# One square, one sum and one root per large piece in a streaming p = 2 pooling kernel

## The chip, the cores and the metric

The kernel runs on one core of a Trainium2 chip. The metric is device time in microseconds (us) of one execution. All times of kernels are medians; a profile is of one single run. A ratio is the mean time of one kernel's runs over that of the other's runs of the same rounds, so it is not quite the ratio of the two medians that stand beside it.

## The reference

```python
x = randn(32, 256, 4096) float32;  p = 2.0;  kernel_size = 4
for i in range(1024):
    window = np.abs(x[:, :, 4*i : 4*i+4]) ** p
    result[:, :, i] = np.mean(window, axis=-1) ** (1.0 / p)
```

For p = 2 each output is the square root of a quarter of the sum of four squares. 134.2 MB are read and 33.6 MB written, and each input element is used once.

## The kernel before

A partition holds 13184 columns of x at a time, in one of three buffers ("slots"). ScalarE squares in place, VectorE adds groups of four into an output buffer, and ScalarE takes roots there. A load fills a slot and is worked on in three pieces. Two loads make a group, which is stored as one block; there are two output buffers. A small odd piece comes first, and the last loads are smaller.

```python
slots = [[(W, [4416, 4384, 4384])]] * 18          # W = 13184: one load, three pieces
slots += [[(6592, [3296, 3296])] * 2, [(6592, [3296, 3296]), (4216, [2112, 2104])]]
X_SLOTS, O_SLOTS = 3, 2
groups = [2] * 9 + [3, 1]
late = {7, 8, 9, 10}                              # these are stored from the sync queue, at the end
FINE, ENDS, LAG = range(22), (), 1                # FINE: loads whose every piece has its own root
PAIRS = 16                                        # from this load on: two adds instead of a reduce
# ... (loads, blocks and buffers cut)
for i in range(n):
    s, _, w, chunks = loads[i]
    while ahead < n and loads[ahead][0] < s + X_SLOTS:
        load(ahead); ahead += 1                   # waits, on the queue, until its slot is free
    # ... (choice of the output buffer cut)
    for step in chunks:
        v = xs[i][:, c:c + step]
        nc.scalar.activation(out=v, in_=v, func=Act.Square)
        total_sum(ots[g][:, summed:summed + step // k], v, i)
        while pending and pending[0][0] <= done - LAG:
            root(*pending.pop(0)[1:])             # a root comes one piece late; at a group's end, the store
        # ... (counting cut)
        if ends or i in FINE or (i in ENDS and c == w):
            pending.append((done - 1, g, ots[g][:, rooted:summed], ends))
```

Of the kernel before, what the change touches and what calls it, by code (L numbers as in the profile page):

```python
# [1 line left out]

# [4 lines left out]


@with_exitstack
def kernel(  # L10
    ctx: ExitStack,
    tc: tile.TileContext,
    x: bass.AP,
    p: float,
    kernel_size: int,
    out: bass.AP,
):








    nc = tc.nc

    assert float(p) == 2.0, "kernel specialized for p == 2"
    k = int(kernel_size)
    assert k == 4, "kernel specialized for kernel_size == 4"  # L30

    P = nc.NUM_PARTITIONS
    fp32 = mybir.dt.float32
    Act = mybir.ActivationFunctionType
    xf = x.rearrange("b c l -> (b c l)")
    of = out.rearrange("b c l -> (b c l)")
    total = xf.shape[0] // P

    W, O_W = 13184, 6592
    X_SLOTS, O_SLOTS = 3, 2  # L40
    slots = [[(W, [4416, 4384, 4384])]] * 18
    slots += [[(6592, [3296, 3296])] * 2, [(6592, [3296, 3296]), (4216, [2112, 2104])]]
    ODD = 840
    groups = [2] * 9 + [3, 1]
    late = {7, 8, 9, 10}
    in_x = {9: (2, 0), 10: (2, 4944)}
    FINE, ENDS, LAG = range(22), (), 1
    PAIRS = 16


    loads = [(s, sum(w for w, _ in slot[:j]), *slot[j]) for s, slot in enumerate(slots)
             for j in range(len(slot))]
    n = len(loads)
    assert sum(w for _, _, w, _ in loads) + ODD == total

    firsts = [sum(groups[:g]) for g in range(len(groups))]
    assert sum(groups) == n
    group_of = [g for g, count in enumerate(groups) for _ in range(count)]
    columns = [sum(w for _, _, w, _ in loads[firsts[g]:firsts[g] + groups[g]])
               for g in range(len(groups))]  # L60

    x_pool = ctx.enter_context(tc.tile_pool(name="x_pool", bufs=1))
    o_pool = ctx.enter_context(tc.tile_pool(name="o_pool", bufs=1))

    x_tiles = [x_pool.tile([P, W], fp32, name=f"xt{j}") for j in range(X_SLOTS)]
    o_tiles = [o_pool.tile([P, O_W], fp32, name=f"ot{j}") for j in range(O_SLOTS)]
    ctx.enter_context(tc.manual_schedule())

    def block(flat, g, div):
        at, width = sum(columns[:g]) * P // div, columns[g] * P // div  # L70
        return flat[at:at + width].rearrange("(p w) -> p w", p=P)

    xs = {}

    def load(i):
        s, at, w, _ = loads[i]
        v = x_tiles[s % X_SLOTS][:, at:at + w]
        g = group_of[i]
        src = sum(loads[j][2] for j in range(firsts[g], i))
        nc.sync.dma_start(out=v, in_=block(xf, g, 1)[:, src:src + w])  # L80
        xs[i] = v

    ots = {}

    def store(g, queue):
        queue.dma_start(out=block(of, g, k), in_=ots[g])  # L86

    def root(g, o, ends):
        nc.scalar.activation(out=o, in_=o, func=Act.Sqrt, scale=1.0 / k)  # L89
        if ends and g not in late:  # L90
            store(g, nc.scalar)

    def total_sum(o, v, i):
        add = mybir.AluOpType.add
        if i < PAIRS:
            nc.vector.tensor_reduce(  # L96
                out=o, in_=v.rearrange("p (n j) -> p n j", j=k),
                axis=mybir.AxisListType.X, op=add,
            )
            return  # L100

        q = v.rearrange("p (n j) -> p n j", j=k)
        front = v[:, 0:v.shape[1] // 2]
        h = front.rearrange("p (n j) -> p n j", j=2)
        nc.vector.tensor_tensor(out=h, in0=q[:, :, 0:2], in1=q[:, :, 2:4], op=add)  # L105
        nc.vector.tensor_tensor(out=o, in0=h[:, :, 0], in1=h[:, :, 1], op=add)  # L106


    Q = 120
    odd = ODD * P // Q  # L110
    t = o_tiles[1][0:Q, 0:odd]
    nc.sync.dma_start(out=t, in_=xf[(total - ODD) * P:total * P].rearrange("(p w) -> p w", p=Q))  # L112
    ahead = 0
    while ahead < n and loads[ahead][0] < X_SLOTS:
        load(ahead)
        ahead += 1
    nc.scalar.activation(out=t, in_=t, func=Act.Square)  # L117
    o = o_tiles[1][0:Q, odd:odd + odd // k]
    nc.vector.tensor_reduce(  # L119
        out=o, in_=t.rearrange("p (n j) -> p n j", j=k),  # L120
        axis=mybir.AxisListType.X, op=mybir.AluOpType.add,
    )
    nc.scalar.activation(out=o, in_=o, func=Act.Sqrt, scale=1.0 / k)  # L123
    nc.scalar.dma_start(
        out=of[(total - ODD) * P // k:total * P // k].rearrange("(p w) -> p w", p=Q), in_=o,
    )
    pending = []
    done = 0
# [3 lines that stand above are left out]
            load(ahead)  # L132
            ahead += 1
        g = group_of[i]
        if i == firsts[g]:
            t, first = (o_tiles[g % O_SLOTS], 0) if g not in in_x else (x_tiles[in_x[g][0]], in_x[g][1])
            ots[g] = t[:, first:first + columns[g] // k]
            summed = rooted = 0
        assert sum(chunks) == w
        c = 0  # L140
        for step in chunks:
            v = xs[i][:, c:c + step]
            nc.scalar.activation(out=v, in_=v, func=Act.Square)  # L143
            total_sum(ots[g][:, summed:summed + step // k], v, i)
            while pending and pending[0][0] <= done - LAG:
                root(*pending.pop(0)[1:])
            done += 1
            c += step
            summed += step // k
            ends = summed == columns[g] // k  # L150
            if ends or i in FINE or (i in ENDS and c == w):
                pending.append((done - 1, g, ots[g][:, rooted:summed], ends))
                rooted = summed
    for job in pending:
        root(*job[1:])
    for g in sorted(late):
        store(g, nc.sync)


# [1 line left out]
_INS = ['x', 'p', 'kernel_size']  # L161
_OUTS = [((32, 256, 1024), 'float32')]

_NUMBERS = {'p': 2.0, 'kernel_size': 4}


# [26 lines left out]
```

## Time and profile before

| | kernel before |
|---|---|
| time, beside the changed kernel | 394.81 us (394.58 to 395.49, 6 runs) |
| span of the profile | 392.8 us |
| packet time of both DMA queues | 99.2% of the time of the core's 16 DMA engines |
| ScalarE (ACT), VectorE (DVE) busy | 292.5 us, 271.8 us |

Read the packet time first, and the engines against it. The last number is the median time in us from issue to landing:

```profile
xt<-in_x_dram SPq DMA_DIRECT2D x18, 6592.0 KB, 39.9
out_dram<-ot ACTq DMA_DIRECT2D x7, 3296.0 KB, 27.6
```

A load has 6592 KB, 128 rows of 52,736 bytes.

### The profile page before, as it was taken

How to read it: one execution, taken by the hardware profiler on the slowest of the kernel's cores; microseconds unless marked ns; L12 is line 12 of the kernel's file. 1: busy time of each engine (PE TensorE's matmuls, PEld its weight loads, DVE VectorE, ACT ScalarE, POOL GpSimd, SP SyncE). 2: the span in 40 equal slices, each digit the busy share in tenths (PEclk: the TensorE clock that was granted, in tenths of full speed). 3: DMA queues.
4: the chain of work that ended last, by engine and by line, in shares of the span. 5: the costliest groups of instructions: out<-in, count | busy, mean ns of one | idle time of the engine just before them, and what ended most of it. 6: DMA issues, size and time to landing. Idle time of an engine off the chain costs nothing.

```text
span 392.8 us, 341 instructions
## 1 busy us (share of the span) xinstructions
DVE 271.8 (69%) x77; ACT 292.5 (74%) x128; POOL 0.2 (0%) x4
## 2 busy tenths in 40 slices
DVE  1059989594959495949594959495949494778781
ACT  3088987776776777677867786868586859899990
POOL 0000000000000000000000000000000000000000
DMA  9999999999999989999999999999999999999997
GB/s 361 420 429 446 446 446 384 430 470 430 389 432 473 430 387 435 467 430 422 432 435 430 427 435 427 430 435 459 459 404 430 459 438 430 395 430 432 429 432 315
DMA packets 5024, 167.79 MB, mean 427 GB/s; under 512 B 558, under 2 KB 678, under 8 KB 926
## 3 DMA queue, kind: packets, MB, share of 16 engines
q1 hardware_dynamic: 3879, 144.04, 85.2%
q10 hardware_dynamic: 1143, 23.73, 14.0%
q14 instruction: 2, 0.02, 0.0%
HBM read 134.22 MB, written 33.55 MB: 427 GB/s over the span
## 4 chain that ended last, share of the span: by engine, by line
DMA 62%; ACT 21%; DVE 10%; issue 4%; SPq 0%; ACTq 0%
DMA xt<-in_x_dram 62%; ACT xt L143 17%; DVE ot L96 8%; ACT ot L89 3%; ACT xt L89 1%; DVE xt L105 1%; DVE xt L106 0%; ACTq L86 0%; SPq L80 0%; SPq L112 0%; ACTq L89 0%
## 5 line engine op out<-in xcount | busy, mean ns | idle before, releaser
L143 ACT ACTIVATE xt<-xt 128x4384 f32<-128x4384 f32 (+4 forms) x62 | 229.6, 3705 | 85.1 <-DMA xt<-in_x_dram 81.9
L96 DVE TENSOR_REDUCE ot<-xt 128x1096 f32<-128x4384 f32 (+1 forms) x48 | 227.0, 4731 | 90.1 <-ACT xt L143 89.8
L89 ACT ACTIVATE ot<-ot 128x1096 f32<-128x1096 f32 (+1 forms) x54 | 59.8, 1107 | 1.8 <-DVE ot L96 1.1
L105 DVE TENSOR_TENSOR xt<-xt 128x1648 f32<-128x1648 f32 (+4 forms) x14 | 28.4, 2032 | 16.0 <-ACT xt L143 16.0
L89 ACT ACTIVATE xt<-xt 128x824 f32<-128x824 f32 (+2 forms) x8 | 6.5, 817 | 1.9 <-DVE xt L106 1.9
L106 DVE TENSOR_TENSOR ot<-xt 128x1096 f32<-128x1096 f32 (+1 forms) x6 | 7.8, 1303 | 0.2
L106 DVE TENSOR_TENSOR xt<-xt 128x824 f32<-128x824 f32 (+2 forms) x8 | 7.5, 939 | 0.3
L119 DVE TENSOR_REDUCE ot<-ot 120x224 f32<-120x896 f32 x1 | 1.1, 1086 | 5.7 <-ACT ot L117 5.7
L117 ACT ACTIVATE ot<-ot 120x896 f32<-120x896 f32 x1 | 0.9, 949 | 2.7 <-DMA ot<-in_x_dram 2.7
L117 ACT ACT_TABLE_LOAD x1 | 1.3, 1283 | 0.7 <-PEq L174 0.7
L123 ACT ACT_TABLE_LOAD x1 | 1.3, 1283 | 0.0
L123 ACT ACTIVATE ot<-ot 120x224 f32<-120x224 f32 x1 | 0.4, 389 | 0.0
L174 POOL MEMSET const-bfloat16-1.0<- 128x1 bf16 x1 | 0.1, 101 | 0.0
L174 POOL MEMSET const-uint8-127<- 128x1 uint8 x1 | 0.1, 101 | 0.0
L174 POOL MEMSET const-float32-0.0<- 128x1 f32 x1 | 0.1, 99 | 0.2 <-issue 0.2
L174 POOL MEMSET const-float32-1.0<- 128x1 f32 x1 | 0.1, 99 | 0.0
## 6 DMA issues: line engine op xcount, KB each, us to landing
xt<-in_x_dram SPq DMA_DIRECT2D x18, 6592.0 KB, 39.9
out_dram<-ot ACTq DMA_DIRECT2D x7, 3296.0 KB, 27.6
xt<-in_x_dram SPq DMA_DIRECT2D x3, 3296.0 KB, 29.4
out_dram<-ot SPq DMA_DIRECT2D x2, 3296.0 KB, 30.0
out_dram<-xt SPq DMA_DIRECT2D x1, 2472.0 KB, 10.4
xt<-in_x_dram SPq DMA_DIRECT2D x1, 2108.0 KB, 26.8
out_dram<-xt SPq DMA_DIRECT2D x1, 527.0 KB, 7.1
ot<-in_x_dram SPq DMA_DIRECT2D x1, 420.0 KB, 4.0
```

What stands on the lines that cost most here:

```text
L89: nc.scalar.activation(out=o, in_=o, func=Act.Sqrt, scale=1.0 / k)
L96: nc.vector.tensor_reduce(out=o, in_=v.rearrange("p (n j) -> p n j", j=k), axis=mybir.AxisListType.X, op=add,)
L105: nc.vector.tensor_tensor(out=h, in0=q[:, :, 0:2], in1=q[:, :, 2:4], op=add)
L106: nc.vector.tensor_tensor(out=o, in0=h[:, :, 0], in1=h[:, :, 1], op=add)
L117: nc.scalar.activation(out=t, in_=t, func=Act.Square)
L119: nc.vector.tensor_reduce(out=o, in_=t.rearrange("p (n j) -> p n j", j=k), axis=mybir.AxisListType.X, op=mybir.AluOpType.add,)
L123: nc.scalar.activation(out=o, in_=o, func=Act.Sqrt, scale=1.0 / k)
L143: nc.scalar.activation(out=v, in_=v, func=Act.Square)
L174: nc = _bacc.Bacc("TRN2", target_bir_lowering=False, num_devices=1)
```

## The change

The intent is to pay the fixed cost of an instruction once for a whole load: one square and one sum for each load, one root for each store. The two-add form of the sum starts one load earlier, at load 15. Waits that follow from others are declared away. The odd piece is squared on VectorE, and its root and store stay on ScalarE.

```diff
-    slots = [[(W, [4416, 4384, 4384])]] * 18
-    slots += [[(6592, [3296, 3296])] * 2, [(6592, [3296, 3296]), (4216, [2112, 2104])]]
+    slots = [[(W, [W])]] * 17 + [[(W, [6592, 6592])]]
+    slots += [[(6592, [6592]), (6592, [6592])], [(6592, [6592]), (4216, [2112, 2104])]]
-    FINE, ENDS, LAG = range(22), (), 1
-    PAIRS = 16
+    FINE, ENDS, LAG = {21}, {19, 20}, 1
+    PAIRS = 15
+    def follows(ins, before):
+        for b in before:
+            tc.declare_no_dep(ins.ins, b.ins, reason="follows from other waits")
... (calls of follows() after each square, sum and root cut)
-    nc.scalar.activation(out=t, in_=t, func=Act.Square)
+    nc.vector.tensor_tensor(out=t, in0=t, in1=t, op=mybir.AluOpType.mult)
```

More of the change, by code (lines that the diff above doesn't have):

```diff
@@ L73 @@
     xs = {}
+    by_load = []
     def load(i):
@@ L83 @@
     ots = {}
+    stores = {}
+    by_act = []
+    sums = []
+    def follows(ins, before):
+        for b in before:
+            tc.declare_no_dep(ins.ins, b.ins, reason="follows from other waits")
     def store(g, queue):
-        queue.dma_start(out=block(of, g, k), in_=ots[g])
+        stores[g] = queue.dma_start(out=block(of, g, k), in_=ots[g])
     def root(g, o, ends):
-        nc.scalar.activation(out=o, in_=o, func=Act.Sqrt, scale=1.0 / k)
+        r = nc.scalar.activation(out=o, in_=o, func=Act.Sqrt, scale=1.0 / k)
+        follows(r, by_act[:-1] + list(stores.values()))
+        by_act.append(r)
         if ends and g not in late:
@@ L95, in total_sum @@
         if i < PAIRS:
-            nc.vector.tensor_reduce(
+            r = nc.vector.tensor_reduce(
                 out=o, in_=v.rearrange("p (n j) -> p n j", j=k),
@@ L99, in total_sum @@
             )
+            follows(r, sums[:-1])
+            sums.append(r)
             return
@@ L104, in total_sum @@
         h = front.rearrange("p (n j) -> p n j", j=2)
-        nc.vector.tensor_tensor(out=h, in0=q[:, :, 0:2], in1=q[:, :, 2:4], op=add)
-        nc.vector.tensor_tensor(out=o, in0=h[:, :, 0], in1=h[:, :, 1], op=add)
+        r = nc.vector.tensor_tensor(out=h, in0=q[:, :, 0:2], in1=q[:, :, 2:4], op=add)
+        follows(r, sums[:-1] + by_load)
+        r = nc.vector.tensor_tensor(out=o, in0=h[:, :, 0], in1=h[:, :, 1], op=add)
+        follows(r, sums[:-1])
+        sums.append(r)
     Q = 120
@@ L123 @@
     nc.scalar.activation(out=o, in_=o, func=Act.Sqrt, scale=1.0 / k)
-    nc.scalar.dma_start(
+    stores["odd"] = nc.scalar.dma_start(
         out=of[(total - ODD) * P // k:total * P // k].rearrange("(p w) -> p w", p=Q), in_=o,
@@ L142 @@
             v = xs[i][:, c:c + step]
-            nc.scalar.activation(out=v, in_=v, func=Act.Square)
+            r = nc.scalar.activation(out=v, in_=v, func=Act.Square)
+            follows(r, by_act[:-1])
+            by_act.append(r)
             total_sum(ots[g][:, summed:summed + step // k], v, i)
```

## The prediction

> **What bounds the kernel now.** I read the page from the top down: busy shares, the 40 slices, the DMA queues, then the chain that ended last.
>
> ```profile
> span 392.8 us, 341 instructions
> DVE 271.8 (69%) x77; ACT 292.5 (74%) x128; POOL 0.2 (0%) x4
> ...
> DMA  9999999999999989999999999999999999999997
> ...
> q1 hardware_dynamic: 3879, 144.04, 85.2%
> q10 hardware_dynamic: 1143, 23.73, 14.0%
> ...
> HBM read 134.22 MB, written 33.55 MB: 427 GB/s over the span
> ...
> DMA 62%; ACT 21%; DVE 10%; issue 4%; SPq 0%; ACTq 0%
> ```
>
> No compute engine is over 74%, while the DMA row has 9 in every slice but two. The packets of the two queues took 85.2 + 14.0 = 99.2% of the time of 16 engines: 389.7 of 392.8 us. The chain line looks as if ScalarE and VectorE carried 31% of the time. That is a trap: the chain runs through the release of an x buffer, which is what let a load be *issued*, but the load then stood in a queue. To see that, I took the DMA view by stretches (after the core's DVE, ACT and POOL columns come clock, DMA share, GB/s) and the chain in order of time:
>
> ```profile
> 10.00:20.00 10.00, 0.00 (x0) 0.00 (x0) 0.00 (x0) 1.00 1.00 430
> 20.00:40.00 20.00, 14.19 (x4) 17.51 (x7) 0.00 (x0) 1.00 0.98 423
> 100.00:150.00 50.00, 37.83 (x8) 35.75 (x17) 0.00 (x0) 1.00 1.01 438
> 382.00:384.00 2.00, 1.85 (x2) 0.62 (x2) 0.00 (x0) 1.00 1.01 432
> 390.00:391.00 1.00, 0.00 (x0) 0.00 (x0) 0.00 (x0) 1.00 0.51 198
> ```
> ```profile
> 51.58 3.88 ACT xt L143
> ...
> 65.56 4.73 DVE ot L96
> 70.29 0.02 issue
> 70.31 39.85 DMA xt<-in_x_dram
> 110.16 0.02 issue
> ```
>
> Between 10 and 20 us nothing computes at all and the rate is 430 GB/s; with both engines at work it is 423 to 438. So compute neither slows the transfers nor feeds them. In the chain a load landed at 51.58, its buffer was free at 70.29 (turnaround 18.7 us), and the next load into it took 39.85 us to land at 110.16. The sum, 58.6 us, is the period of three buffers: 19.5 us for each load. Of the 39.85 us a load therefore spends some 20 waiting behind its predecessor.
>
> **What the Trainium skill says.** "DMA: Bandwidth & Descriptors", section "Where 436 GB/s comes from", gives 435 GB/s as the ceiling of the fabric; the trace agrees, with 427 over the whole span and about 431 between the first packet and the last. Its section "Queues, rings and completion order" says that each DMA engine takes turns between the queues packet by packet; that fits the stores, which need 27.6 us for 3296 KB beside loads, though alone they would need about 8. "ScalarE: Activation LUTs", "What ACT_TABLE_LOAD costs", gives 186 ns + 0.833 ns per element for an ACTIVATE with immediate operands, and about 93 ns of overlap back to back. "VectorE: DVE Perf Modes", "The perf-mode tier table", has tensor_reduce and fp32 tensor_tensor both at one element a cycle. The forms agree:
>
> ```profile
> L96 DVE TENSOR_REDUCE ot<-xt 128x1096 f32<-128x4384 f32 x32 | 151.0, 4719 | 6.3 <-ACT xt L143 6.0
> L143 ACT ACTIVATE xt<-xt 128x4384 f32<-128x4384 f32 x36 | 138.4, 3843 | 3.3 <-ACT ot L89 3.3
> L89 ACT ACTIVATE ot<-ot 128x1096 f32<-128x1096 f32 x36 | 39.7, 1103 | 0.2
> L105 DVE TENSOR_TENSOR xt<-xt 128x1648 f32<-128x1648 f32 x6 | 11.3, 1875 | 3.9 <-ACT xt L143 3.8
> ```
>
> 3843 is 186 + 0.833 x 4384 (3838); 4719 is 4384/0.96 + 152; 1875 is (1648 + 151)/0.96.
>
> **The change, part by part.**
> *Fewer, larger instructions.* Squares go from 62 to 24 and roots from 62 to 13, by the program order of the changed kernel: 87 fewer at 0.186 us is 16 us of ScalarE, less the overlap that was hidden already, so 12 to 14 us: 292.5 becomes about 279. On VectorE 48 reduces become 15 of 13184/960 + 0.152 = 13.9 us (208 us), and with the packed adds the sum is about 264, from 271.8. None of it lies on the path that sets the end while DMA is 99.2% busy: worth 0 there.
>
> *Turnaround.* A load is now squared in 11.2 us (186 + 0.833 x 13184 ns) before its one sum of 13.9 us can start: 25.1 us instead of 18.7, because the pieces no longer overlap each other. By the period above, issue to landing falls to 58.6 - 25.1 = 33.5 us, of which 19.5 is the load's own turn. The queue ahead of it shrinks from 20 to 14 us and does not empty. Cost: 0. The start is tighter, as the first three loads come without a store: load 0 landed at 20.36 and load 2 at 51.58. The buffer of load 0 is free at 20.4 + 25.1 = 45.5, and the packet records show 1.8 us from an issue to its first packet (odd piece: 0.73 to 2.56). So load 3 can start at 47.3, some 4 us before the engines run dry.
>
> *Engine order.* The root of a pair (186 + 0.833 x 6592 = 5.7 us) now follows the square of the next load: 11.2 + 5.7 = 16.9 us of ScalarE against 19.5 a load, and VectorE has 13.9. Neither falls behind. A store issued 16.9 us after a landing has until 2 x 19.5 + 11.2 = 50.2, so 33 us, before the sum two groups later wants its buffer. The median store needs 27.6; the longest of the trace 34.2, where VectorE would lose 1 us out of 5.6 spare.
>
> *Waits declared away.* With 0.02 us between steps of the chain ("issue" lines), on engines with a quarter of their time idle: 0.
>
> *Odd piece.* One table load (1.28 us) and one square leave ScalarE. Its first real work waits for load 0 at 20.36 with 12.97 us idle before it, so: 0.
>
> *Tail.* This is where the end could move. In before, the packets of the store of 2472 KB start back to back at 383.88, though it was issued at 380.26: 3.6 us of queue, 1.8 of it slack beyond the issue latency. In the changed kernel ScalarE squares load 16 from 325.0 to 336.2, then does, from the root of loads 14 and 15 on, seven pieces of 5.7 us to some 375.5 (root, two squares of load 17, square 18, root, squares 19 and 20). The adds of load 20 (3.6 + 1.9) end at 381.0, its root (1.56) at 382.5, and the store goes out then, 2.2 us late; overlap of back-to-back ACTIVATEs may give back 0.7. Its packets start at 383.6 to 384.3 instead of 383.9: a hole of 0 to 0.4 us. The last store goes out at about 387.0 instead of 384.8, yet its packets waited until 389.74 in before: no loss. Sum of all parts: +0.2 us.
>
> **Rivals.**
> *Compute is the bound and the 16 us count.* For it: the chain's 21% ACT and 10% DVE. Against it: 99.2% of packet time, and 39.9 us to land a load of which half is queue. Even if every hole closed, the 389.7 us of packets and the 1.8 us between span and measured time leave 391.5, or 0.9% off; 2% would need 387.1.
> *The longer turnaround starves the queue.* A new wait of the loads on the sum would appear as DMA idle. For it: 6.4 us more on every buffer, in order engines, store and sum tied by one buffer. Against it: 14 us of queue left, 4 at the start. To make 2% (7.9 us) the turnaround would have to exceed about 58.6 - 19.5 - 1.8 = 37 us throughout; if only load 3 is late, it costs 1 to 3 us.
> *The coarse tail exposes compute.* ScalarE is the busy engine after 340 us. If my tail walk is short by 2 us, the end moves by 2 us: 397, still within 2%.
> *A better head or tail.* About 2.5 us before the first packet and 1 at the end are fixed by latency, and the last pieces are as small as before, so a gain of more than 1 us is unlikely.
>
> **Range and chances.** The before time of 395.0 plus 0.2 is 395.2. Run to run it varied by 0.45. Below, a luckier start or fewer gaps between packets may give 1.2; above, one of the two small holes costs at most 1 to 2. So 394.0 to 396.5 eight times in ten. Faster by 2% would break the packet time: 1%. Slower by 2% needs starvation in the steady part: 2%. The rest, 97%, is the same.
>
> **What would show it.** DMA share of both queues again at 99%; ScalarE near 279 and VectorE near 264 us; loads issued to landing at 33 to 34 us instead of 39.9; squares of 11.2 us, reduces of 13.9 us; the store of 2472 KB issued near 382, and time to landing shorter than 10.4 us. The prediction is wrong if the DMA row shows slices under 9 in the middle (starvation), if a slice rate beyond 440 GB/s holds up (the transfer rate depends on compute after all), or if the last 10 us show the engines waiting for a root.

## The result, and the profile after

| | before | changed |
|---|---|---|
| time | 394.81 us (6 runs) | 395.58 us (393.85 to 395.82, 6 runs) |
| ratio, 95% interval | | 1.0011 (0.9992 to 1.003) |
| the same kernel run again, beside before | 394.67 us (11 runs) | 394.87 us (394.04 to 395.61, 6 runs) |
| ratio of that, 95% interval | | 1.0003 (0.9989 to 1.0017) |

The two kernels take the same time. From the page of the changed kernel, the lines that answer to those shown of before:

```profile
span 393.8 us, 182 instructions
...
DVE 262.9 (67%) x35; ACT 279.7 (71%) x39; POOL 0.2 (0%) x4
...
DMA  9999999999989999999999999999999999999996
...
q1 hardware_dynamic: 3879, 144.04, 85.0%
q10 hardware_dynamic: 1143, 23.73, 14.0%
...
xt<-in_x_dram SPq DMA_DIRECT2D x18, 6592.0 KB, 31.6
out_dram<-ot ACTq DMA_DIRECT2D x7, 3296.0 KB, 27.0
```

The instructions fall from 341 to 182, ScalarE's busy time by 12.8 us and VectorE's by 8.9 us. The DMA row is as full as before (one slice in its middle shows an 8 in either kernel), and the packets again take 99% of the span. Loads now land 31.6 us (median) after their issue instead of 39.9. They are issued later, because a buffer is free later, and stand in the queue for less time. From the list of waits, first of the kernel before, then of the changed one (waiter, what it waited for, us in total, times, longest):

```profile
ACT xt L143 <- DMA xt<-in_x_dram: 81.9, 18, 13.0
```
```profile
ACT xt L162 <- DMA xt<-in_x_dram: 97.7, 14, 12.9
```

That is where the saved time went: ScalarE waits 15.8 us longer for loads, after 12.8 us less of work. The end of the timeline (start, duration, then what; in brackets how long the engine was idle before, and what ended that) shows the tail, first one line of the kernel before, then the changed kernel:

```profile
380.26 4.88 SPq L86 DMA_DIRECT2D out_dram<-xt  x2
```
```profile
380.92 1.58 ACT L101 ACTIVATE xt<-xt 128x1648 f32<-128x1648 f32 x1 [0.78 <-DVE xt L123]
382.09 0.71 DVE L123 TENSOR_TENSOR xt<-xt 128x528 f32<-128x528 f32 x1
382.40 1.94 ACT L162 ACTIVATE xt<-xt 128x2104 f32<-128x2104 f32 x1
382.52 4.88 SPq L98 DMA_DIRECT2D out_dram<-xt  x2
```

The root of load 20 ends at 382.50, and the store that needs it goes out at 382.52, against 380.26 in the kernel before.

### The profile page after: what moved, and what is told of

Read it like the earlier page. It is cut to its first block, busy times and chain, and to the rows that moved or that the text cites. A ratio compares the mean times of both kernels' runs of the same rounds, so it can differ in the third digit from the quotient of the medians.

```text
span 393.8 us, 182 instructions
## 1 busy us (share of the span) xinstructions
DVE 262.9 (67%) x35; ACT 279.7 (71%) x39; POOL 0.2 (0%) x4
## 4 chain that ended last, share of the span: by engine, by line
DMA 48%; ACT 34%; DVE 16%; SPq 0%; ACTq 0%; issue 0%
DMA xt<-in_x_dram 48%; ACT xt L162 27%; DVE ot L110 14%; ACT ot L101 6%; DVE xt L121 1%; DVE xt L123 1%; ACT xt L101 1%; ACTq L98 0%; SPq L81 0%; SPq L131 0%
## 5 line engine op out<-in xcount | busy, mean ns | idle before, releaser
L162 ACT ACTIVATE xt<-xt 128x13184 f32<-128x13184 f32 (+3 forms) x24 | 222.2, 9272 | 99.4 <-DMA xt<-in_x_dram 97.7
L110 DVE TENSOR_REDUCE ot<-xt 128x3296 f32<-128x13184 f32 x15 | 208.3, 13886 | 94.7 <-ACT xt L162 94.7
L101 ACT ACTIVATE ot<-ot 128x6592 f32<-128x6592 f32 x9 | 51.1, 5682 | 0.0
L121 DVE TENSOR_TENSOR xt<-xt 128x3296 f32<-128x3296 f32 (+3 forms) x9 | 34.5, 3835 | 23.8 <-ACT xt L162 23.5
L123 DVE TENSOR_TENSOR ot<-xt 128x3296 f32<-128x3296 f32 (+1 forms) x4 | 10.9, 2734 | 0.1
L101 ACT ACTIVATE xt<-xt 128x3296 f32<-128x3296 f32 (+3 forms) x4 | 5.8, 1449 | 2.3 <-DVE xt L123 2.3
L123 DVE TENSOR_TENSOR xt<-xt 128x1648 f32<-128x1648 f32 (+2 forms) x5 | 7.0, 1408 | 0.2
L136 DVE TENSOR_TENSOR ot<-ot 120x896 f32<-120x896 f32 x1 | 1.1, 1093 | 4.7 <-DMA ot<-in_x_dram 4.7
## 6 DMA issues: line engine op xcount, KB each, us to landing
xt<-in_x_dram SPq DMA_DIRECT2D x18, 6592.0 KB, 31.6
```

Source lines behind the costliest of these rows:

```text
L101: r = nc.scalar.activation(out=o, in_=o, func=Act.Sqrt, scale=1.0 / k)
L110: r = nc.vector.tensor_reduce(out=o, in_=v.rearrange("p (n j) -> p n j", j=k), axis=mybir.AxisListType.X, op=add,)
L121: r = nc.vector.tensor_tensor(out=h, in0=q[:, :, 0:2], in1=q[:, :, 2:4], op=add)
L123: r = nc.vector.tensor_tensor(out=o, in0=h[:, :, 0], in1=h[:, :, 1], op=add)
L136: nc.vector.tensor_tensor(out=t, in0=t, in1=t, op=mybir.AluOpType.mult)
L162: r = nc.scalar.activation(out=v, in_=v, func=Act.Square)
```

## The experiments

Two theories stood against each other. The first: transfers are the bound, and both what the change saves (fixed costs) and what it adds (a longer turnaround) lie beside them. The second: compute or its waits bear on the end, and gain and loss happen to cancel. In the first case the time must follow the bytes, and both costs must come out once transfers or buffers no longer cover them. A *turnaround* is the time from the landing of a load to the end of its last sum, when its buffer is free.

### Fewer bytes to write

Both kernels store only half of each block's columns. The result is incomplete, and the arithmetic is all there.

```diff
-        queue.dma_start(out=block(of, g, k), in_=ots[g])
+        queue.dma_start(out=block(of, g, k)[:, 0:columns[g] // k // 2], in_=ots[g][:, 0:columns[g] // k // 2])
```

The kernel before, then the changed kernel:

> The kernel before storing half of each block's columns (result incomplete on purpose, arithmetic unchanged): 16.8 MB less, at 431 GB/s 38.9 us. Theory: 355 to 358 us. Rival (compute is the bound, with 292 us of ScalarE and its waits): over 380 us.

> The changed kernel storing half. Theory: again the bytes alone, 355 to 359 us, within 0.5% of the kernel before with half stores, as the buffers' period of 3 x 17.6 us still holds 25.1 + 17.6 + 2. Rival (the longer turnaround begins to starve the loads): over 362 us.

Measured: 360.29 us for the kernel before and 361.12 us for the changed kernel, beside 394.75 us for the unaltered kernel before. Both miss their range, by 2 us each, and still fall by 34 of the expected 39 us, with the same ScalarE and VectorE work as ever (291.7 and 279.6 us of ScalarE). They lie 0.2% apart, as expected. The packet time of the kernel before fell from 389.7 us (99.2% of 392.8) to 351.4 us (98.0% of 358.6), which is the whole 38.3. The rest is in the tail. With half the stores, too few bytes are left to cover the last pieces: the DMA share between 350 and 355 us was 0.28 in the kernel before and 0.61 in the changed one. By the packet records laid over one another, the DMA engines stood idle for 5.0 and 5.7 us between 345 and 357.3 us, and for less than 0.1 us between 10 and 345 us. So the time follows the bytes up to the tail, and the tail was covered by stores before.

### Few bytes to read: what the saved time is worth when it counts

Every load is cut to a quarter of its columns. The buffers are filled with zeros first, so that nothing reads what was not written. The result is wrong, and the arithmetic and the stores stay.

```diff
-        nc.sync.dma_start(out=v, in_=block(xf, g, 1)[:, src:src + w])
+        nc.sync.dma_start(out=v[:, 0:w // 4], in_=block(xf, g, 1)[:, src:src + w // 4])
+    # one memset on VectorE and two on GpSimd: x_tiles[j][:, W // 4:W] = 0.0
```

> The kernel before with every load cut to a quarter of its columns (buffers filled with zeros first, result wrong on purpose, all arithmetic and all stores kept): 67 MB instead of 168, 156 us of packet time at 431 GB/s. Theory (transfers are the bound, compute lies under them): compute is now what is left, ScalarE's 292 us back to back plus some 10 us of head and 10 of tail, so 305 to 315 us, DMA share near 50%. Rival (compute already sets the end of the kernel before): little change, over 380 us.

> The changed kernel with the same cut. Theory: here the fixed costs that it saves count, ScalarE 280 us instead of 292, so 8 to 16 us less than the kernel before with the same cut, some 295 to 305 us. Rival (the saved time is eaten by the coarser pipeline itself, whatever the transfers do): within 2 us of the other, or more.

Measured: the kernel before 314.54 us, in its range. The changed kernel took 328.34 us, 13.8 us *more* where 8 to 16 less were expected. The first theory's account of the bound holds, with 67 MB the kernel before runs at the pace of ScalarE (93% busy). Its account of the change did not: the larger pieces lose more than the fixed costs they save. The timeline of the changed kernel with quarter loads shows how, in one round of two loads:

```profile
59.44 22.27 ACT L165 ACTIVATE xt<-xt 128x13184 f32<-128x13184 f32 x2 [0.45 <-ACT ot L104]
70.66 27.68 DVE L113 TENSOR_REDUCE ot<-xt 128x3296 f32<-128x13184 f32 x2 [3.60 <-ACT xt L165]
84.58 5.70 ACT L104 ACTIVATE ot<-ot 128x6592 f32<-128x6592 f32 x1 [2.87 <-DVE ot L113]
90.31 0.34 ACTq L101 DMA_DIRECT2D out_dram<-ot  x1
90.69 22.27 ACT L165 ACTIVATE xt<-xt 128x13184 f32<-128x13184 f32 x2 [0.41 <-ACT ot L104]
```

The first square of the pair (11.2 us from 59.44) must end before its sum (13.9 us from 70.66) starts. The root of that sum starts at 84.58, and ScalarE, done with its second square at 81.71, waits 2.87 us for it. The next pair starts at 90.69. So square, sum, root and the issue of the store are a loop of 31.25 us for two loads, though ScalarE has only 28.0 us of work in it. Over the run this is the wait of roots for sums, here in the kernel before, then in the changed one, both with quarter loads:

```profile
ACT ot L92 <- DVE ot L99: 1.1, 1, 1.1
```
```profile
ACT ot L104 <- DVE ot L113: 22.8, 7, 5.6
```

In the kernel before it is 1.1 us in total, as a root comes one *small* piece late. ScalarE has 12.2 us less of work in the changed kernel (279.4 instead of 291.6) and 21.7 us more of this wait. It also idles 3.3 us longer at the head, and that is of the experiment's own making: the odd piece's square, which the change moved to VectorE, stands there behind a zero-fill of 8.3 us. The first large square starts at 14.37 us instead of 13.23, so about 1.1 of the 13.8 us come from this.

If that loop is the cause, letting the root come one square later must end it:

```diff
-    FINE, ENDS, LAG = {21}, {19, 20}, 1
+    FINE, ENDS, LAG = {21}, {19, 20}, 2
```

> The changed kernel with quarter loads, and each root one square later (LAG 2 instead of 1), so that ScalarE does not wait for the sum in front of it. Theory (with LAG 1 one square, its sum and its root make a loop, 11.2 + 13.9 + 5.7 + 0.4 = 31.3 us for two loads, where ScalarE has 28.1 us of work): the 22.8 us that ScalarE waited before its roots go, 300 to 310 us against 328, and so below the 314.5 of the kernel before. Rival (the lost time lies in the squares and sums themselves): within 5 us of 328.

Measured: 313.75 us, 14.6 less than with LAG 1. The waits before roots are gone. The time is 4 us above the range and only just below the 314.54 of the kernel before, because two other waits came, and the head stayed as it was. From its list of waits:

```profile
ACT xt L165 <- DMA xt<-in_x_dram: 8.1, 3, 2.8
DVE ot L113 <- DMA out_dram<-ot: 6.7, 3, 2.5
```

So the loop is shown as the main cause of the 13.8 us. That the saved 12.8 us of ScalarE bring a gain anywhere is not shown: even here, where compute is the bound, they went into new waits.

### LAG 2 with full loads

> The changed kernel with full loads and LAG 2. Theory (there the loop is hidden, so nothing is gained, and the store goes out 19.5 us later, 36 us after the landing, and has 14 us before the sum that wants its buffer, where it needs 27): VectorE waits for stores, every second turnaround grows from 25 to 38 us, at the limit of the three buffers: 396 to 412 us. Rival (stores have room, time is the bytes alone): 394 to 396 us.

Measured: 404.39 us, ratio 1.0252 (1.0239 to 1.0265) to the kernel before, as the theory expects. The edit that gave 14.6 us with few bytes costs almost 10 with all of them. The store goes out one square later, the sum two groups on waits for it to leave the output buffer, and the x buffer of that sum is held (for 30 to 44 us in three of four loads, where LAG 1 had 25 to 27):

```profile
DVE ot L110 <- DMA out_dram<-ot: 56.4, 3, 20.3
```

Such a line is absent from the waits of the changed kernel with LAG 1. There the store had room: it was issued 16.8 us after the landing and landed 27.0 us later (median), before the sum at about 49. Only a part of the loss is idle time of the DMA engines. Between the two profiles (402.5 and 393.8 us) their time outside packets grew by 4.0 us, and their packet time, for the same bytes, by 4.7 us (394.6 instead of 389.9). Why the packets took longer is not known.

### Two x buffers instead of three: what the longer turnaround costs

```diff
+    ROT = 2
-        v = x_tiles[s % X_SLOTS][:, at:at + w]
+        v = x_tiles[s % ROT][:, at:at + w]
... (the two conditions that load ahead use ROT as well; the third buffer serves the tail's outputs only)
```

> The kernel before with two x buffers in rotation instead of three. Theory (two load periods must hold the turnaround of 18.7 us, 1.8 us of issue and the load's own 16 to 20 us): 37 to 41 us against 39 that the transfers need, so just starved: 400 to 425 us. Rival (turnaround is of no account to the transfers at all): 395 us.

> The changed kernel with two x buffers. Theory: the turnaround of 25.1 us makes 43 to 47 us for two loads, so 430 to 470 us, 25 to 40 us more than the kernel before with two, with holes in the DMA row. This is the cost that three buffers hide. Rival (coarse pieces cost nothing): as the kernel before with two buffers, within 2%.

Measured, with a correct result: 430.26 us and 448.62 us, ratios 1.0919 and 1.1366 to the unaltered kernel before. Starvation appears in both, and more of it with the longer turnaround: outside their packets the DMA engines had 25 us of the span in one and 43 us in the other, against 3 us with three buffers. The rest of either loss, some 13 us, is packet time: the same bytes took 403 us instead of 389.7. Why is not known. The second is in its range; the first is 5 us above its own, so the gap is 18 us and not 25 to 40. The chains in order of time (start, duration, what) tell why. The kernel before with two buffers, then the changed one:

```profile
122.26 3.89 ACT xt L144
126.17 4.76 DVE ot L97
130.96 1.12 ACT ot L90
132.08 3.76 ACT xt L144
135.86 4.73 DVE ot L97
140.61 24.09 DMA xt<-in_x_dram
```
```profile
107.61 11.20 ACT xt L163
118.83 13.90 DVE ot L111
132.74 18.22 DMA xt<-in_x_dram
```

Turnaround and landing add up to 18.4 + 24.1 = 42.5 us in one and 25.1 + 18.2 = 43.3 us in the other. Over the middle of the run the period of two loads was 42.8 us in the first (80.03 to 336.55 in six periods) and 43.6 us in the second (64.01 to 369.19 in seven). I had left out that a load beside a store is slower. In the first kernel stores run beside loads (29.6 us each in the median, and the load needs 24). In the second they fall into the hole that the turnaround leaves (9.2 us each), and the load has the engines to itself. The steady part made about 7 of the 18 us. The rest arose at the two ends: load 2 was squared from 64.01 instead of 57.05, and some 4 us came after load 16.

The rival that coarse pieces cost nothing falls. With three buffers the same 6.4 us of turnaround cost nothing that could be measured.

### Parts of the change, and the tail

The first run of the changed kernel was 0.77 us above the kernel before. Three variants looked for these 0.77 us. The first gives the fine pieces back from load 17 on, the second puts the declared-away waits back, and the third takes the odd piece out and gives its columns to the last load.

```diff
# a_finetail
-    slots = [[(W, [W])]] * 17 + [[(W, [6592, 6592])]]
-    slots += [[(6592, [6592]), (6592, [6592])], [(6592, [6592]), (4216, [2112, 2104])]]
-    FINE, ENDS, LAG = {21}, {19, 20}, 1
+    slots = [[(W, [W])]] * 17 + [[(W, [4416, 4384, 4384])]]
+    slots += [[(6592, [3296, 3296])] * 2, [(6592, [3296, 3296]), (4216, [2112, 2104])]]
+    FINE, ENDS, LAG = range(17, 22), (), 1
# a_waits
-            tc.declare_no_dep(ins.ins, b.ins, reason="follows from other waits")
+            pass
# a_noodd, on top of a_finetail: ODD = 0, last load (5056, [2528, 2528]), code of the odd piece removed
```

> The changed kernel with the pieces of the kernel before from load 17 on (thirds and halves, a root for each). Theory (the changed kernel loses its 0.5 to 1 us at the coarse tail, where the store of 2472 KB goes out at 382.5 instead of 380.3): that store is issued at 380.0 to 380.8, the hole at 382 to 384 us goes, span 392.5 to 393.2, ratio to the kernel before 0.997 to 1.000. Rival (the difference is noise or lies in the steady part): ratio 1.001 to 1.003 as for the changed kernel.

> The changed kernel with the declared-away waits put back; instructions and their order are the same. Theory (waits that are always fulfilled cost nothing on idle engines): the time of the changed kernel, ratio 1.000 to 1.003, ScalarE and VectorE busy times within 0.5 us of it. Rival (each extra wait costs on the way): over 1.005.

> The fine-tail kernel without the odd piece: its 840 columns go to the last load (5056 columns). Theory (only bytes and badly filled packet time count): the 3584-byte packets took 205 ns, 0.6 us of the engines more than at the full rate, and 0.1 us for the 896-byte ones, so 0.5 to 1 us less than the fine-tail kernel, ratio to the kernel before 0.996 to 0.999, if the larger last piece stays hidden. Rival (the last piece is exposed): 0.5 to 1 us more than the fine tail.

> The changed kernel once more, unaltered. Theory (its runs fall into two groups about 1.2 us apart, as those of the variant with the waits kept did, 394.3 and 395.6, and which one comes is chance at the tail): some runs near 394.3, median between 394.2 and 395.7. Rival (the coarse tail costs a steady 0.7 us): all runs between 395.3 and 395.9, interval above 1.001.

| | time, us | runs | ratio to before, 95% interval |
|---|---|---|---|
| changed kernel, first | 395.58 | 6 | 1.0011 (0.9992 to 1.003) |
| fine tail | 395.08 | 6 | 1.0005 (0.999 to 1.002) |
| waits kept | 394.42 | 6 | 1.0001 (0.9987 to 1.0015) |
| no odd piece | 395.87 | 5 | 1.0026 (1.0014 to 1.0038) |
| changed kernel, again | 394.87 | 6 | 1.0003 (0.9989 to 1.0017) |

The runs of the kernel with the waits kept were 394.20, 394.33, 394.39, 394.45, 395.53 and 395.69. Those of the changed kernel, run again, were 394.04, 394.05, 394.24, 395.50, 395.53 and 395.61. They fall into two groups some 1.3 us apart, with nothing in between. In its first rounds the changed kernel had five runs in the upper group and one at 393.85. So the 0.77 us were mostly a matter of which group came up. The rival, a steady 0.7 us for the coarse tail, falls.

Where the 1.3 us lie can be read from the two profiles of this kernel, as the first is of a run in the upper group (395.62 us) and the second of one in the lower (394.24 us). Up to the landing of load 15 they agree within 0.3 us (load 15: 301.20 and 301.17). Load 16 landed at 324.10 in one and at 322.72 in the other, and all that follows is as much later. Each transfer ends with sixteen packets of 4 bytes, which are taken here as one from each DMA engine. By these packets, one engine finished its part of load 16 1.8 us after the last but one (0.3 us in the lower run). At the end of the upper run it still wrote eight rows of 0.16 us each, until 392.40, while the other fifteen were done at 390.76. In the lower run all sixteen were done at 391.03. So in these two profiles the group is one DMA engine that fell behind and never caught up. Why it fell behind is not known, and there is one profile of each group.

The waits cost nothing measurable: VectorE's busy time is 262.9 us and ScalarE's 279.7 us with them and without them.

The fine tail was a miss in its mechanism: its store of 2472 KB went out at 381.96, not at 380.0 to 380.8, because ScalarE still came late from the large square and root in front of load 17. (The profiled run, 394.18 us, is a fast one; the changed kernel's own store went out at 381.13 in a run like it.) Its ratio was in neither of the two ranges that I had set, and its interval holds both 1 and the ratio of the changed kernel, so it tells nothing about the coarse tail.

Taking the odd piece out was a miss as well. Load 0 could be squared at 19.84 us instead of 20.28, so about 0.4 us were won at the start, but they did not reach the end: the kernel is 0.26% slower than before, and 0.8 us slower than the fine tail, which is in the rival's range. Its store of 2472 KB was issued at 382.52, no earlier than in the changed kernel, and its DMA share was still 0.89 between 390 and 391 us, where the fine tail's was down to 0.34. In its profile, too, one DMA engine ended 0.8 us after the other fifteen. How much of the loss is the larger last piece, and how much such an engine, stays open.

## Why the prediction was right

*The bound.* The packets again took 99.0% of the span, and cutting 38.3 us of packet time took 34 us off either kernel. Laid over one another, the packets left the 16 DMA engines idle for less than 0.1 us of the 370 us from 10 to 380, in both kernels. This step held.

*Fewer, larger instructions.* Predicted were some 279 and 264 us of busy time, measured 279.7 and 262.9. Their worth of 0 on the path was right too: the time went into waits for loads (81.9 to 97.7 us).

*Turnaround.* The square measured 11.19 us and the reduce 13.89 us, and from landing to the free buffer 12 of the first 15 loads took 25.2 us, as worked out. The other three (25.9 to 26.8 us) began their square only after a root and a store (in the timeline, load 3 started at 68.78 right behind them, though it had landed at 67.12). Issue to landing was put at 33.5 us. The median is 31.6, but loads 6 to 17 took 30 to 32 and 35 to 37 us in turn, 33.3 us in the mean, so the sum was right and only its evenness was not foreseen. At the start, load 3 was issued at 45.42 us (45.5 predicted) and its packets followed those of load 2 without a hole. That the turnaround has a price at all was shown by the two-buffer runs.

*Engine order.* "Neither falls behind" held, since 31.25 us for two loads is under the 39 that transfers need. But the check compared each engine's work for a load (16.9 us for ScalarE where a root falls due, 13.9 us for VectorE) with the 19.5 us that a load takes. It did not see that square, sum and root form a loop, 3.2 us longer for two loads than ScalarE's work in it. Where transfers do not cover this, with quarter loads, an expectation built on work alone said 8 to 16 us less and met 13.8 us more. The room for the store was right: with LAG 1 no sum waited for a store, and with LAG 2, which used up that room, the time rose by 10 us.

*Waits and odd piece.* Both were put at 0, and the variant with the waits kept gave 1.0001. Moving the odd piece's square was not tried alone, nor was the two-add form of load 15.

*Tail.* The store of 2472 KB was expected at 382.5 and went out at 382.52. That it fits so closely is partly luck: in the second profile of the same kernel, without the late DMA engine, the line is

```profile
381.13 4.88 SPq L98 DMA_DIRECT2D out_dram<-xt  x2
```

Its time to landing fell from 10.4 to 9.1 us, as expected. The hole of 0 to 0.4 us measured 0.1 us between 383 and 384 us in the first profile, and nothing in the second, by the packet records laid over one another. (The DMA share of a stretch of 2 us cannot show it, as `prof` counts a packet's whole time where it starts: 382 to 384 us shows 0.87 in one profile and 0.88 in the other, followed by 1.13 and 1.06.) The prediction's packet times are all read 0.8 us too late: by the packet records the odd piece's first packet started at 1.75 us and not at 2.56, the store's at 383.07 and not at 383.88, the last store's at 388.93 and not at 389.74. From issue to first packet it is thus about 1.0 us and not 1.8 (0.8 for this store in the changed kernel), and the queue in front of the store was 2.8 us and not 3.6. The slack of 1.8 us on which the estimate rests is the difference of the two and stands. The sum of +0.2 us agrees with the second series (394.87 against 394.67) and is below the first (0.77), where the upper group of runs prevailed. None of these differences is clear of noise.

*Signs of being wrong.* The DMA row has one 8 in its middle, as before, without idle engines behind it. Single slices reach 474 GB/s (470 before), but over stretches of 40 to 50 us the rate was 423 to 445. The third sign, a wait for a root near the end, is there in the small: the store left as soon as the root ended, and this is the hole of 0.1 us.

*Rivals.* "Compute is the bound" fell with the half stores. "The queue starves" was real, but one buffer away. "The coarse tail exposes compute" would have needed 2 us, and at most 0.1 was there.

No version here beats both kernels by a margin that could be measured. The lowest single run of all kernels with the full work was 393.85 us, and the packet time alone is 389.7.

## What to carry to other kernels

Add up the packet time of the DMA queues before anything else; if it fills the span, an engine's saved time turns into waits for loads, however much of the chain that ended last carries that engine's name. Then check what the change spends: here turnaround of a buffer and the slack of a store, which were free only because three input buffers gave a load 58.6 us, and two output buffers gave a store about 33 us. When pieces grow, look at the loop that the engines make among themselves (square, sum, root of one piece) and not only at the work of each, and do not carry over, without a run, the setting that is best when compute is the bound: LAG 2 cost 10 us here when transfers were.

## What the Trainium skill lacked or had wrong

- "Trainium Kernel Development and Optimization", section "Best Practices", says to double-buffer for performance. Two input buffers took 430.26 us here (448.62 with the large pieces), three 394.6. The page has no rule for how many buffers; what served here was that their joint period must hold the turnaround, the issue and the load's own transfer.
- "DMA: Bandwidth & Descriptors", section "Where 436 GB/s comes from", says that for transfers between HBM and SBUF the HBM side (about 358 GB/s) binds. Read as a general rule that does not hold here: this core moved 427 GB/s over the whole span, near the 435 that the same section gives for the fabric. The page's section "Measured (HBM→SBUF, 128 partitions, SWDGE, issued from GpSimd)" ties the 358 to both cores of a pair streaming, which the first section leaves out. The runs do not show what the other core of the pair did.
- "VectorE: DVE Perf Modes", section "The perf-mode tier table", has no time for tensor_reduce beyond its rate. The runs show 4719 ns for 4384 fp32 elements and 13,886 ns for 13,184, that is one element a cycle at 0.96 GHz and about 152 ns. The same sum as two tensor_tensor adds took 7.03 + 3.59 = 10.6 us.
- No page told of the two groups of run times, 1.3 us apart, into which the runs of two of these kernels fell with the clock at 1.0 throughout. In one profile of each group the difference is one of the 16 DMA engines, which ended 1.6 us after the other fifteen (392.40 against 390.76).
